# Output projection's weight sums: from accumulating DMAs to VectorE adds, two jobs behind their loads

## The chip, the cores and the metric

The kernel runs on one core of one Trainium2 chip. The metric is the device time of one execution in microseconds (us). Three runs of the kernel before gave a median of 634.77 us (634.74 to 635.29).

## The reference

One decoder block on 512 tokens of width 1024: RMSNorm, one input projection, an mLSTM branch (`ya`) and a sparse-attention branch (`yb`), each projected to width 1024, merged by sigmoid gates, then an output projection, a residual and a final RMSNorm. What matters here is the end:

```
merged = sigmoid(g_a) * (ya @ w_branch_a) + sigmoid(g_b) * (yb @ w_branch_b)
x = x + merged @ w_out
return rmsnorm(x, final_norm_g)
```

`w_branch_a` and `w_out` are 1024 x 1024, everything is float32, `merged` is 512 x 1024.

## The kernel before

**Products.** Each float32 operand is split into a high and a low part (`split`: ACT copies the high part to a rounded type, DVE subtracts it from the source), and a product is three matmuls: high by high, low by high, high by low.

**Branch A.** `branch(GA, j, ...)` computes the 128 columns of output block j for all 512 tokens: 8 x 3 = 24 matmuls into one PSUM bank of the ring `pp` (three banks). There are eight such jobs, in the order of blocks 0, 4, 1, 5, 2, 6, 3, 7; they are called jobs 1 to 8. A job's `load` asks SP for two things: the gate `s` (256 KB, ring of three buffers) and the weights `wr` (512 KB, ring of three), which are split at once into `wh` on ACT and `wl` on DVE (rings of four). The `Stream` loads two jobs ahead, so the load and the split of job k+2 are traced just before job k's matmuls. After the matmuls DVE does the *gating* of the job, `s = (s + 1) * bank`, and the *merge add*, `mB = s + mB`; the merge add frees the `s` buffer. `merge` then settles the block of the job before (`settle`: split into `meh` on ACT and `mel` on DVE), and after blocks 4, 5 and 6 forms sums of two blocks by four small DVE operations (`merged_sums`) and splits them into `mSh` and `mSl`.

**Output projection.** It is one level of Strassen-Winograd over quarters. The weights `w_out` fall into four quarters B11, B12, B21, B22 of 512 x 512, each in two tiles of 128 x 1024 numbers. Needed are also T3 = B12 + B22, T2 = T3 + B11, T4 = B21 + T2 and T1 = B11 + B12. Seven products follow in fixed order: M11 (with B11), M12 (B21), M22 (T4), MS2 (T2), MS3 (T3), MS1 (T1), MS4 (B22), 24 matmuls each. M11 reads blocks 0 to 3 of `merged` in turn, for tokens 0 to 127 and then 128 to 255; M12 blocks 4 to 7; M22 the other tokens.

**Weight sums before.** SP loads B12 straight into T3's tiles (`T`) and B22 into `R` tiles, and POOL issues two DMAs that accumulate B22 onto T3 (`added`). B11 is loaded, B12 a second time into `R` tiles, then B21. T2 is two DVE adds (`plus`), T1 two accumulating DMAs on POOL, T4 two DVE adds between M11 and M12 in the text. The calls `stream.run()`, which trace one job each, stand between these.

**What sets the order.** The text is traced once; the framework then places the instructions of each engine by its own estimate of when their operands are ready, earlier text first. Each engine and each DMA queue works its list strictly in order. `tc.keep_in_program_order(ins)` pins an instruction behind the one traced just before it on its engine. The set `ordered` names the engines on which all are pinned: it is emptied early in the kernel, and "pe" is added after the eight jobs, so in this stretch neither DVE nor ACT is pinned; SP and POOL never are.

Line 79 in the profile is the helper through which all PE, ACT and DVE instructions go, so tiles tell them apart. SP's loads are line 143 (weights), 1125 (`s`) and 1284 (`w_out`); POOL's accumulates are 1289 (weight sums) and 1330 (`aside`, output parts onto `xo`).

Of the kernel before, what the change touches and what calls it, by code (L numbers as in the profile page):

```python
# [15 lines left out]
OP = mybir.AluOpType  # L16
AX = mybir.AxisListType.X

T = 512
# [43 lines left out]
def build(  # L63
# [7 lines left out]
    class Engine:  # L71
# [3 lines left out]
        def __getattr__(self, op):  # L75
# [7 lines left out]

            return call

    pe, pool = Engine(nc.tensor, "pe"), nc.gpsimd
    act, dve = Engine(nc.scalar, "act"), Engine(nc.vector, "dve")
    A = act.activation
# [40 lines left out]
    def split(src, hi, lo, eng="a"):  # L129
        if eng == "a":  # L130
            A(hi, src, AF.Copy)
        elif eng == "p":
            pool.tensor_scalar(hi, src, 1.0, 1.0, OP.mult, OP.mult)
        else:
            dve.tensor_copy(hi, src)
        dve.tensor_tensor(lo, src, f(hi), OP.subtract)
# [3 lines left out]
    def weights(src, eng="a"):  # L140
        nk, n = src.shape[1], src.shape[2]
        raw = wp.tile([128, nk, n], F32, name="wr", tag="wr", bufs=3)
        nc.sync.dma_start(raw, src)
        hi = wp.tile([128, nk, n], F32R, name="wh", tag="wh", bufs=4)
        lo = wp.tile([128, nk, n], F32R, name="wl", tag="wl", bufs=4)
        split(raw, hi, lo, eng)
        return hi, lo
# [51 lines left out]
    def passes(ps, lh, ll, rh, rl, nk):  # L199
        for k in range(nk):  # L200
            a, b, c, d = lh(k), ll(k), rh(k), rl(k)
            pe.matmul(ps, a, c, start=k == 0, stop=False)
            yield
            pe.matmul(ps, a, d, start=False, stop=False)
            yield
            pe.matmul(ps, b, c, start=False, stop=k == nk - 1)
            if k < nk - 1:
                yield
# [17 lines left out]
    stream = Stream(2)  # L226
# [50 lines left out]
    def hilo(qs):  # L277
        out = []
        for q in qs:
            hi = wp.tile([128, 2, 512], F32R, name="wh", tag="wh", bufs=4)  # L280
            lo = wp.tile([128, 2, 512], F32R, name="wl", tag="wl", bufs=4)
            split(q, hi, lo)
            out.append((hi, lo))
        return out

    with tc.tile_pool(name="ph0", bufs=2, side="right") as p0, tc.tile_pool(
# [23 lines left out]
        for hf in range(2):  # L310
            ps = PS()
# [126 lines left out]
        split(b, *parts["S1"])  # L438
        split(d, *parts["S4"])

    def plus(dst, a, b):
        for d, x, y in zip(dst, a, b):
            dve.tensor_tensor(d, x, y, OP.add)
        return dst

    def product(banks, k, ws, start=True, tbs=(0, 1), cs=slice(0, 512)):
        ah, al = parts[k]
        for tb in tbs:
            ts = slice(tb * 128, tb * 128 + 128)
            for c in range(4):  # L450
                wh, wl = (w[:, c % 2, cs] for w in ws[c // 2])
                first, last = start and c == 0, c == 3
                m = lambda l, r, first=False, last=False: pe.matmul(
                    banks[tb][:, cs], l, r, start=first, stop=last, skip_group_check=True
                )
                m(ah[:, c, ts], wh, first)
                m(ah[:, c, ts], wl)
                m(al[:, c, ts], wh, False, last)
# [3 lines left out]
    def winograd(qs, target, sink, between=(), w1=None):  # L462
# [26 lines left out]
        Z = [PP() for _ in range(2)]  # L489
        w2 = hilo(b21)  # L490
        t3 = plus(WS(), b12, b22)
        do("t3")
        t2 = plus(WS(), t3, b11)
        do("t2")
        product(Z, "A12", w2)
# [7 lines left out]
        z = keep(X, "kz")  # L503
        w7 = hilo(t3)
        t4 = plus(t2, t2, b21)
        product(X, "S3", w7, False)
        do("P7")
# [130 lines left out]
    load = lambda: next(more)  # L638
# [467 lines left out]
    def branch(base, j, yh, yl, nk):  # L1106
        def gen(w):
            o = 0 if nk == ND else (j % 2) * 128
            ps = PP()
            yield from passes(  # L1110
                ps, lambda k: w[0][:, k, o : o + 128], lambda k: w[1][:, k, o : o + 128],
                lambda k: yh[:, k], lambda k: yl[:, k], nk,
            )
            s = halves.pop((base, j))
            if base == GB:
                if not merged:
                    merged.append(pers.tile([128, ND, T], F32, name="mB", tag="hTh"))
                dve.scalar_tensor_tensor(merged[0][:, j], s, 1.0, ps, OP.add, OP.mult)
            else:
                dve.scalar_tensor_tensor(s, s, 1.0, ps, OP.add, OP.mult)  # L1120
                merge(j, s)

        def load():
            halves[base, j] = sgp.tile([128, T], F32, name="s", tag="s")
            nc.sync.dma_start(halves[base, j], gD[base, j])
            if nk == ND:
                return weights(wav[:, :, j * 128 : j * 128 + 128])
            if j % 2 == 0:
                halves["w"] = weights(wbv[:, :, j * 128 : j * 128 + 256])
            return halves["w"]  # L1130

        stream.add(load, gen)
# [10 lines left out]
    for h in range(4):  # L1143
# [34 lines left out]
        for tb in range(NT):  # L1178
            po = PT()
            for sb in range(tb + 1):  # L1180
                a = KOFF[sb] + (tb - sb) * 128
# [49 lines left out]
    with tc.tile_pool(name="fin", bufs=1, reuse_waits="tile") as fp:  # L1231
# [10 lines left out]
        def merged_sums(i):  # L1242
            a, b = merged[0][:, i], merged[0][:, i + 4]
            a1, a2, b1, b2 = a[:, :256], a[:, 256:], b[:, :256], b[:, 256:]
            dve.tensor_tensor(b2, a2, b2, OP.subtract)
            dve.tensor_tensor(a2, a1, a2, OP.subtract)
            dve.tensor_tensor(a1, b2, a1, OP.subtract)
            dve.tensor_tensor(b1, a1, b1, OP.add)
            sums_split(i, a, 0)
# [9 lines left out]
        def settle():  # L1259
            j = waiting.popleft()  # L1260
            m = merged[0][:, j]
            split(m, meh[:, j], mel[:, j])
            return j

        def merge(j, s):
            m = merged[0][:, j]
            dve.tensor_tensor(m, s, m, OP.add)
            waiting.append(j)
            if len(waiting) > 1:
                k = settle()  # L1270
                if k in (4, 5, 6):
                    merged_sums(k - 4)
# [5 lines left out]
        def tiles(tag, bufs):  # L1278
            return [fp.tile([128, 2, 512], F32, name=tag, tag=tag, bufs=bufs) for _ in range(2)]

        def load(i, j, ts):
            for n, t in enumerate(ts):
                ks = slice(i * 4 + n * 2, i * 4 + n * 2 + 2)
                nc.sync.dma_start(t, wov[:, ks, j * 512 : j * 512 + 512])
            return ts

        def added(ts, more):
            for t, m in zip(ts, more):
                pool.dma_start(t, m, accum_op=OP.add)
            return ts  # L1290

        t3 = load(0, 1, tiles("T", 4))
        b22 = load(1, 1, tiles("R", 8))
        added(t3, b22)
        stream.run()
        b11 = load(0, 0, tiles("R", 8))
        stream.run()
        b12 = load(0, 1, tiles("R", 8))
        stream.run()
        b21 = load(1, 0, tiles("R", 8))  # L1300
        stream.run()
        t2 = plus(tiles("T", 4), t3, b11)
        stream.run(2)
        t1 = added(b12, b11)
        w1 = hilo(b11)
        stream.run()
        settle()
# [40 lines left out]
        L, R = slice(0, 512), slice(512, 1024)  # L1348
# [25 lines left out]
        aside(X, 0, 0, 0, 0.5)  # L1374
        Z = [PP() for _ in range(2)]
        t4 = plus(b21, b21, t2)
        w4 = hilo(t4)
        product(Z, "M12", w2)
        merged_sums(3)
# [65 lines left out]
```

## Time and profile before

| | |
|---|---|
| median of three runs | 634.77 us |
| profiled execution | 637.34 us, span of its instructions 635.3 us |
| mean granted TensorE clock | 0.992 |
| busy: PE, DVE, ACT, POOL | 96%, 78%, 54%, 9% |
| read from HBM | 62.35 MB |

One execution is recorded by the hardware profiler; times are from the span's start. A row of the timeline has start, length, engine, line, operation, output and inputs by tile names, the count, and in brackets how long the engine stood idle before it and what ended that. SPq and POOLq are the parts of those engines that issue DMAs. The "chain of waits" is followed back from the last instruction to what released each step.

### The profile page before, as it was taken

The page shows a single profiled execution, that of the slowest core. Times are in us where ns is not written, and L with a number is a line of the kernel's source. Part 1 is how long each engine was busy: PE and PEld are TensorE (multiplying, and loading weights), DVE is VectorE, ACT ScalarE, POOL GpSimd, SP SyncE. Part 2 cuts the span into 40 slices and gives each one's busy share as a digit, 9 for nine tenths or more (in the row PEclk, how much of TensorE's full clock was granted, in tenths as well). Part 3 has the DMA queues.
Part 4 walks back from the last instruction along what each step waited for, and adds up shares of the span by engine and source line. Part 5 has one row for each costly group of instructions (what it writes and reads, how often), then busy time and mean ns, then how long its engine had stood idle before and what let it go on. Part 6 is the DMA issues. An engine that isn't in the chain of part 4 may idle for free.

```text
span 635.3 us, 8633 instructions
## 1 busy us (share of the span) xinstructions
PE 608.0 (96%) x3014; PEld 502.5 (79%) x3014; DVE 494.0 (78%) x962; ACT 345.9 (54%) x650; POOL 59.1 (9%) x124
## 2 busy tenths in 40 slices
PE   5999999999999999999999999999999999987995
PEld 3988878888888877888888788887878788866784
DVE  4799979596685777876868676989898986459966
ACT  5645457554442456665665665666565643125564
POOL 4000000000000001221312130000000000100120
PEclk9999999999999999999999999999999999999898
DMA  7925644502067442131322213513232337993324
GB/s 240 336 92 165 214 134 122 173 5 83 18 176 197 107 127 83 51 84 50 84 57 77 84 39 97 146 36 99 67 100 67 100 116 200 297 249 105 111 50 150
DMA packets 83643, 76.02 MB, mean 120 GB/s; under 512 B 4960, under 2 KB 64516, under 8 KB 83600
## 3 DMA queue, kind: packets, MB, share of 16 engines
q1 hardware_dynamic: 82016, 71.53, 37.5%
q0 software_dynamic: 1440, 3.67, 3.3%
q8 instruction: 24, 0.39, 0.3%
q10 hardware_dynamic: 144, 0.26, 0.1%
q14 instruction: 19, 0.16, 0.1%
HBM read 62.35 MB, written 8.39 MB: 111 GB/s over the span
## 4 chain that ended last, share of the span: by engine, by line
PE 67%; DVE 16%; DMA 5%; ACT 5%; issue 4%; POOL 1%; SPq 1%; POOLq 0%; ACTq 0%; DVEq 0%
PE pp L79 38%; PE ps L79 16%; PE pt L79 10%; PE po L79 3%; DVE u L79 3%; DVE wl L79 2%; ACT wh L79 2%; DMA T<-R 1%; DMA R<-w_out 1%; DVE mB L79 1%; DMA wr<-w_branch_a 1%; DVE Dm L79 1%; DMA xt<-x 1%; DVE Sl L79 1%; DVE Th L79 1%
## 5 line engine op out<-in xcount | busy, mean ns | idle before, releaser
L79 PE MATMUL pp<-hTh,wh 128*128 128x512 f32 (+1 forms) x360 | 142.6, 396 | 0.0
L79 PE MATMUL pp<-hTl,wh 128*128 128x512 f32 (+1 forms) x360 | 140.0, 389 | 0.0
L79 PE MATMUL pp<-hTh,wl 128*128 128x512 f32 (+1 forms) x360 | 139.8, 388 | 0.0
L79 ACT ACTIVATE wh<-wr 128x1024 fp32r<-128x1024 f32 x56 | 59.0, 1058 | 59.2 <-PE pp L79 43.9
L79 DVE TENSOR_TENSOR wl<-wr,wh 128x1024 fp32r<-128x1024 f32 x56 | 68.2, 1219 | 17.0 <-ACT wh L79 16.9
L79 PEld LDWEIGHTS pp<-hTh,wl 128*128 128x128 f32 x360 | 67.7, 188 | 13.1
L79 PEld LDWEIGHTS pp<-hTh,wh 128*128 128x128 f32 x360 | 67.8, 188 | 10.6
L79 PEld LDWEIGHTS pp<-hTl,wh 128*128 128x128 f32 x360 | 67.9, 189 | 9.9
L959 POOL TENSOR_SCALAR P<-P,st 128x128 f32<-128x128 f32 (+1 forms) x64 | 34.6, 560 | 160.9 <-DVE st L79 69.0
L79 DVE TENSOR_TENSOR wl<-R,wh 128x1024 fp32r<-128x1024 f32 x28 | 33.9, 1221 | 12.8 <-ACT wh L79 12.7
L79 DVE TENSOR_TENSOR wl<-T,wh 128x1024 fp32r<-128x1024 f32 x28 | 33.8, 1222 | 10.4 <-ACT wh L79 10.4
L79 ACT ACTIVATE P<-P,st 128x128 f32<-128x128 f32 (+3 forms) x64 | 35.5, 555 | 11.2 <-DVE st L79 10.7
L79 ACT ACTIVATE pth<-pt 128x512 fp32r<-128x512 f32 (+1 forms) x64 | 26.9, 434 | 25.9 <-PE pt L79 14.6
L79 DVE TENSOR_TENSOR ptl<-pt,pth 128x512 fp32r<-128x512 f32 (+1 forms) x64 | 29.9, 485 | 14.2 <-ACT pth L79 13.7
L79 DVE CUSTOM_DVE_ANT_0 P<-ps,cst 128x128 f32<-128x128 f32 (+3 forms) x64 | 30.5, 487 | 12.7 <-PE ps L79 12.5
L79 ACT ACTIVATE wh<-R 128x1024 fp32r<-128x1024 f32 x28 | 29.1, 1054 | 16.3 <-PE pt L79 7.1
L79 DVE SCALAR_TENSOR_TENSOR u<-pp,prm,u 128x511 f32<-128x511 f32 (+2 forms) x48 | 35.7, 744 | 0.2
L79 ACT ACTIVATE wh<-T 128x1024 fp32r<-128x1024 f32 x28 | 29.1, 1055 | 12.1 <-PE ps L79 5.6
L79 PE MATMUL ps<-k,Th 128*128 128x256 f32 (+2 forms) x112 | 29.1, 341 | 1.4 <-PE pp L79 0.8
L79 PE MATMUL pt<-cst,P 128*128 128x128 f32 x160 | 28.4, 277 | 0.9 <-DVE ptl L79 0.8
L79 PEld LDWEIGHTS pt<-cst,P 128*128 128x128 f32 x160 | 19.7, 140 | 10.9 <-DVE ptl L79 5.8
L79 PE MATMUL pp<-yah,wh 128*128 128x512 f32 x64 | 25.0, 391 | 2.1 <-ACT wh L79 2.1
(350 smaller groups left out, 1392.6 us busy)
## 6 DMA issues: line engine op xcount, KB each, us to landing
wr<-w_in SPq DMA_DIRECT2D x44, 512.0 KB, 4.0
R<-w_in SPq DMA_DIRECT2D x24, 512.0 KB, 4.6
gD<-sg SPq DMA_DIRECT2D x16, 256.0 KB, 2.0
s<-gD SPq DMA_DIRECT2D x16, 256.0 KB, 5.8
wr<-w_branch_a SPq DMA_DIRECT2D x8, 512.0 KB, 4.1
R<-w_out SPq DMA_DIRECT2D x8, 512.0 KB, 9.5
vD<-cq SPq DMA_DIRECT2D x8, 256.0 KB, 3.7
wr<-vD SPq DMA_DIRECT2D x4, 512.0 KB, 4.1
```

The source lines that it names most:

```text
L79: ins = fn(*args, **kw)
L959: pool.tensor_scalar(pj, pj, st[:, 2, j : j + 1], 1.0, OP.mult, OP.mult)
```

## The change

T3 is now computed by DVE from B12 and B22, which are each loaded once into `R` tiles. The loads stand one job apart (B12 before job 1, B22 after it, B11 after job 2, B21 after job 4); T3's adds are traced after job 3, T2's after job 5, and both pairs are pinned. T1 is still accumulated by POOL's DMAs, but traced after T4's adds. The gating and the merge add of the branch-A jobs are pinned too, so each gating stands behind the DVE instruction traced just before it.

```
+    keep = tc.keep_in_program_order
...
-    def plus(dst, a, b):
+    def plus(dst, a, b, held=lambda ins: ins):
         for d, x, y in zip(dst, a, b):
-            dve.tensor_tensor(d, x, y, OP.add)
+            held(dve.tensor_tensor(d, x, y, OP.add))
         return dst
...
-                dve.scalar_tensor_tensor(s, s, 1.0, ps, OP.add, OP.mult)
+                keep(dve.scalar_tensor_tensor(s, s, 1.0, ps, OP.add, OP.mult))
                 merge(j, s)
...
-            dve.tensor_tensor(m, s, m, OP.add)
+            keep(dve.tensor_tensor(m, s, m, OP.add))
...
-        t3 = load(0, 1, tiles("T", 4))
+        b12 = load(0, 1, tiles("R", 8))
+        stream.run()
         b22 = load(1, 1, tiles("R", 8))
-        added(t3, b22)
         stream.run()
         b11 = load(0, 0, tiles("R", 8))
         stream.run()
-        b12 = load(0, 1, tiles("R", 8))
+        t3 = plus(tiles("T", 4), b12, b22, keep)
         stream.run()
         b21 = load(1, 0, tiles("R", 8))
         stream.run()
-        t2 = plus(tiles("T", 4), t3, b11)
-        stream.run(2)
-        t1 = added(b12, b11)
+        t2 = plus(tiles("T", 4), t3, b11, keep)
+        stream.run()
         w1 = hilo(b11)
         stream.run()
         settle()
...
         t4 = plus(b21, b21, t2)
+        t1 = added(b12, b11)
         w4 = hilo(t4)
```

## The prediction

> **What bounds the kernel now.** I read the busy table and the chain of waits first, then the PE rows from 568 us on, then the DVE and SP rows just ahead of each PE stall, and last tables by stage. Jobs are numbered by order: branch-A job 1 is output block 0, then blocks 4, 1, 5, 2, 6, 3, 7 are jobs 2 to 8.
>
> ```profile
> span 635.3 us, 8633 instructions
> PE 608.0 (96%) x3014; PEld 502.5 (79%) x3014; DVE 494.0 (78%) x962; ACT 345.9 (54%) x650; POOL 59.1 (9%) x124
> ...
> PE 67%; DVE 16%; DMA 5%; ACT 5%; issue 4%; POOL 1%; SPq 1%; POOLq 0%; ACTq 0%; DVEq 0%
> ```
>
> TensorE is the bound over the whole span; a change to the weight sums can only win where PE stands still. The timeline of PE shows that place (start, length, idle before it and its releaser):
>
> ```profile
> 567.96 0.39 PE L79 MATMUL pp<-yah,wl 128*128 128x512 f32 x1
> 570.41 0.50 PE L79 MATMUL pp<-yah,wh 128*128 128x512 f32 x1 [2.07 <-ACT wh L79]
> 571.67 0.50 PE L79 MATMUL pp<-yah,wl 128*128 128x512 f32 x1 [0.53 <-DVE wl L79]
> ...
> 584.04 0.39 PE L79 MATMUL ps<-wh,mel 128*128 128x512 f32 x1
> 587.61 0.80 PE L79 MATMUL ps<-wh,meh 128*128 128x512 f32 x1 [3.18 <-ACT meh L79]
> ...
> 594.22 0.40 PE L79 MATMUL pp<-wh,meh 128*128 128x512 f32 x1
> ...
> 599.70 0.39 PE L79 MATMUL pt<-wh,meh 128*128 128x512 f32 x1
> ...
> 605.14 0.39 PE L79 MATMUL ps<-wh,mSh 128*128 128x512 f32 x1
> ```
>
> From 599.70 to 605.14 PE runs the 24 matmuls of M22 without a stop: 5.44 us, 0.227 each. Job 6's last matmul starts at 567.96, so job 7 was due at 568.19. Between 568.19 and 599.70 stand 96 matmuls (jobs 7 and 8, M11, M12), 21.76 us of work in 31.51 us. **PE loses 9.75 us here**: 2.07 and 0.53 because job 7's weights are late, 3.18 because block 3 of the merged activations is late, and then a slow clock: from 587.61 to 594.22 the 15 remaining matmuls of M11 take 6.61 us instead of 3.40, so 3.21 more. The other 0.76 is pipeline restart around the three gaps.
>
> Why are the weights and block 3 late? The DVE timeline:
>
> ```profile
> 541.18 0.69 DVE L79 SCALAR_TENSOR_TENSOR s<-s,pp 128x512 f32<-128x512 f32 x1 [3.35 <-PE pp L79]
> ...
> 552.57 1.23 DVE L79 TENSOR_TENSOR T<-T,R 128x1024 f32<-128x1024 f32 x1 [8.23 <-DMA T<-R]
> 553.71 0.68 DVE L79 SCALAR_TENSOR_TENSOR s<-s,pp 128x512 f32<-128x512 f32 x1
> ...
> 555.44 0.68 DVE L79 TENSOR_TENSOR mB<-s,mB 128x512 f32<-128x512 f32 x1
> ...
> 570.39 1.23 DVE L79 TENSOR_TENSOR wl<-wr,wh 128x1024 fp32r<-128x1024 f32 x1 [6.61 <-ACT wh L79]
> ...
> 574.70 0.68 DVE L79 SCALAR_TENSOR_TENSOR s<-s,pp 128x512 f32<-128x512 f32 x1
> ...
> 585.01 0.68 DVE L79 SCALAR_TENSOR_TENSOR s<-s,pp 128x512 f32<-128x512 f32 x1
> ```
>
> The gatings (`s<-s,pp`) are those of jobs 1, 2, 5 and 7. At 24 matmuls a job, PE finished job 2 at about 546.4, job 5 at 562.7. Gating 2 starts 7 us late: ahead of it in DVE's queue stood the first add of T2 = T3 + B11, which waited 8.23 us for the DMA that accumulates B22 onto T3. Its releaser, in the chain of waits:
>
> ```profile
> 534.65 8.60 DMA R<-w_out
> ...
> 543.88 8.66 DMA T<-R
> ```
>
> A load of 8.60 us, then an accumulate of 8.66. The late gating then goes round through SP (and ACT, last row):
>
> ```profile
> 533.69 0.91 SPq L1284 DMA_DIRECT2D T<-w_out  x2
> ...
> 536.46 1.08 SPq L1125 DMA_DIRECT2D s<-gD  x1
> ...
> 543.01 0.98 SPq L1284 DMA_DIRECT2D R<-w_out  x2
> 556.15 0.34 SPq L1125 DMA_DIRECT2D s<-gD  x1
> 556.53 1.85 SPq L1284 DMA_DIRECT2D R<-w_out  x2
> 558.49 0.53 SPq L143 DMA_DIRECT2D wr<-w_branch_a  x1
> 560.34 3.59 SPq L1125 DMA_DIRECT2D s<-gD  x1
> 564.03 0.39 SPq L143 DMA_DIRECT2D wr<-w_branch_a  x1
> ...
> 569.30 1.06 ACT L79 ACTIVATE wh<-wr 128x1024 fp32r<-128x1024 f32 x1 [7.80 <-DMA wr<-w_branch_a]
> ```
>
> The `s` ring has three buffers; job 5's sits in SP's queue until job 2's merge (555.44 + 0.68) frees one at 556.12. Quarter B21 and job 7's weights stand behind it. Those weights are asked for at 558.49 and split at 569.30, 10.8 us later, on a crowded DMA. DVE's second stall (6.61) is this same load, with gating 5 queued behind it 12 us after its matmuls. From there DVE has a backlog that puts gating 7 at 585.01, 8.6 us after PE finished job 7, and M11 stops on block 3. One cause, all 9.75 us.
>
> **The change part by part.** DMA first: the queues in a window, then two stages (us, PE, PEld, DVE, ACT, POOL busy, clock, DMA share).
>
> ```profile
> DMA packets 5926, 9.62 MB, mean 278 GB/s; under 512 B 331, under 2 KB 2225, under 8 KB 5924
> q1 hardware_dynamic: 5348, 7.50, 64.3%
> q0 software_dynamic: 576, 2.10, 34.0%
> ...
> 533.60:568.20 34.60, 34.60 (x154) 28.41 (x152) 16.90 (x24) 7.57 (x10) 3.70 (x4) 1.00 0.99 278
> 568.20:599.70 31.50, 25.73 (x97) 19.88 (x97) 28.57 (x43) 16.59 (x23) 1.74 (x2) 0.89 0.45 133
> ```
>
> The DMA engines are full (0.99) from 533.6 to 568.2. Plain transfers took 64.3% of 34.6 us, 22.2 us for 7.50 MB: 3.0 us per MB. POOL's four accumulates (T3's two, T1's two) took 34.0%, 11.8 us for 2.10 MB: 5.6 us per MB.
>
> *Removed.* The second load of B12 (two SP issues, 1.05 MB): 3.1 us of DMA time. T3's accumulate (two POOL issues, 1.05 MB): 5.9 us. So 9.0 of 34.6 us of DMA work go, and the full stretch should end near 559 instead of 568. The 8.23 us DVE wait goes with them. What is late next: the plain loads of B12 and B22.
>
> *Added.* T3 = B12 + B22 on DVE: two adds of 1.23, so 2.45 us. They are pinned behind the last DVE instruction traced before them, the merged-sum split of jobs 1 and 2, which can't precede merge 2, about 547.9. Loads asked for from 533.7 to 538 and landing in 8.60 are there by 547. I take no wait.
>
> *Moved: T2's adds*, same two, now behind the split that follows job 4 (PE end 557.3). B11 is then asked for behind job 4's `s`, about 543, and is there by 552. *B22, B11 and B21* go one job later in program order, so in SP's queue each may stand one `s` further back: B22 behind 536.5, B11 behind 542.6, B21 behind merge 2 or 3 (547.9 or 553.4). Even the last leaves B21 twenty us before its split.
>
> *Weights.* With merge 2 at 547.9 instead of 556.1, job 7's weights are asked for between 550 and 556. Charged with the worst landing above, 10.8, they come at 561 to 567; with 7.54, the chain's price for job 8's, at 558 to 564. PE needs them split (1.06 + 1.23) at 568.2, so landed by 565.9. I take 562, the 7.54 from the middle of that window, since the DMA is less full than when 10.8 was paid: both first gaps go.
>
> *Pinned gating.* Each gating now can't pass the instruction traced just before it, which is the weight split of the job two later (or a quarter's split); the merge add is pinned behind the gating. That wait is new by name; the 570.39 row shows that the order was already so there. Queued behind it are merge, `s` load and weights. With weights at 562, gating 5 (PE end 562.7) waits at most about 2 us, and the PSUM bank it holds is wanted by job 8 only at 573.6: hidden. Uncovered, it costs what the 570.39 row costs.
>
> *T1's accumulate* is traced after T4's adds, on POOL, which has nothing else from 547 to 592; it may float up as soon as T3 has read B12, or stand beside the first output accumulates. It is wanted by the split at 609.47, 9.75 earlier in new time, 599.7. Bounds: 0 to 0.87 (one POOL issue ahead of the output accumulates, their row below), or a gain of its 5.9 us of DMA time off the full stretch. I take 0.
>
> ```profile
> 609.47 1.06 ACT L79 ACTIVATE wh<-R 128x1024 fp32r<-128x1024 f32 x1 [0.81 <-PE ps L79]
> ...
> 592.54 0.87 POOL L1330 DMA_DIRECT2D xo<-late  x1 [34.89 <-ACT late L79]
> ```
>
> *Is DVE able to carry it?* Its busy time from job 1's gating until T4's splits are done:
>
> ```profile
> 541.10:568.20 27.10, 14.23 (x21) 1.00 1.00 279
> 568.20:597.90 29.70, 26.84 (x40) 0.89 0.47 139
> ```
>
> 41.07 us, with T3 43.5. New time allows 541.1 to 588.15, 47.05 us. It fits with 3.5 us to spare, so DVE is 92% loaded and its order matters. I give back one wait of the smallest size seen, 0.53.
>
> **Sum.** 9.75 - 0.53 = 9.2 us. Against the profiled execution, 637.34 us (span 635.3): 628.1. That execution stands 2.57 above the median 634.77; nothing in its rows says the 9.75 would differ, so on the median: **625.5 us**.
>
> A page on the clock: the Trainium skill, TensorE: Matmul & The Clock Gate, section What's actually happening, puts the drop to half clock after at least one idle window of about 3.4 us. Here 2.07 us of idle left the clock alone and 3.18 cost it. By that rule 3.18 is a borderline case, and an execution that escaped it would have 3.2 less to win, 628.7. The three runs lie within 0.6 us of each other, so I go by the row. It also says that a leftover wait near 2 us should stay cheap.
>
> **The rivals.** *A, partial:* the weights are on time, but DVE's 92% is met in a bad order and M11 still stops for block 3. For it: the 3.5 us of slack, and gating 7 standing behind both splits of B11. Against: block 3 is not wanted until 9 matmuls into M11, 581.1, 7.5 us after job 7's end. If all of 3.18 + 3.21 and its restart stay, only some 3.0 of the 9.75 is won, 631.8; if under 2 us, about 627.
>
> *B, no change:* DVE waits for a plain w_out load where it waited for the accumulate. The load alone took 8.60. For it to hold gating 2 back as before, B22 would have to land near 552, so be asked for at 543 or later, and T3 would have to stand before gating 2, which its pin forbids. 634.8.
>
> *C, slower:* the pin ties gating to weights and the three `s` buffers tie weights to gating. If SP keeps job 7's weights behind job 7's `s`, they wait for merge 4 (558.8): landing with 10.8 at 570, gating 5 after their split, 572.3; merge 5 at 573.6 frees job 8's `s` and weights, landing with 7.54 at 581.5, split 583.8. Job 7 runs from 572.3 (4.1 us idle, half clock, 3.2 more), job 8 from 583.8 to 589.3, M11 and M12 to 600.2, and T2's 2.45 now lies inside the jam: 602.6 against 599.70, so about 637.7. It decides when job 7's weights land after about 569. Against: before, they were asked for ahead of the `s` of two jobs, and the DMA has 9.0 us less to do.
>
> **How the numbers follow.** Full recovery 0.53 (its own range 623.8 to 627.0); A 0.23 (627 to 633.4); B 0.09; C 0.15. 0.2% of 634.8 is 1.3 us, about what measurement tells from no change: faster 0.76, same 0.09, slower 0.15. Below, at most one more wait could go with fewer transfers, DVE's for an output accumulate:
>
> ```profile
> 622.14 0.42 DVE L79 SCALAR_TENSOR_TENSOR xo<-pp,xo 128x256 f32<-128x256 f32 x1 [1.67 <-DMA xo<-late]
> ```
>
> 625.5 less 1.67 is 623.8. Above, the range takes in A and the better half of B: 634.9.
>
> **What would show it.** Right: no `T<-R` on POOL; two `T<-R,R` adds after 548 with little idle; gating 2 near 547; job 7's weights asked for before 557; no PE idle over 1 us from 568 to 600; M22 starting near 590 and no 0.43 us spacing in M11. Wrong: DVE idle of several us before a weight split or a T add, with a gating right behind it; SP holding weights behind an `s` load past 558; an `meh` wait still in M11; or T1's accumulate among the output accumulates with DVE waiting on `xo<-late`.

## The result and the profile after

| | before | after |
|---|---|---|
| median, us | 634.75 (633.47 to 635.29, 4 runs) | 626.14 (625.76 to 626.62, 4 runs) |
| ratio | | 0.9868, 95% interval 0.985 to 0.9885 |
| profiled execution; span, us | 637.34; 635.3 | 626.62; 624.8 |
| mean granted clock | 0.992 | 0.997 |
| read from HBM | 62.35 MB | 61.30 MB |

The forecast was 625.5 us; the measurement stands 0.6 us above it. From the page of the changed kernel, the busy table and the chain's shares by engine:

```profile
span 624.8 us, 8626 instructions
PE 604.0 (97%) x3014; PEld 501.3 (80%) x3014; DVE 496.2 (79%) x964; ACT 345.5 (55%) x650; POOL 57.5 (9%) x122
...
PE 75%; DVE 13%; ACT 5%; issue 3%; DMA 1%; POOL 1%; SPq 0%; POOLq 0%; ACTq 0%; DVEq 0%
```

DMA's share of the chain falls from 5% to 1%, PE's rises from 67% to 75%. The chain of waits (start, length, engine or transfer) now runs through the whole branch A on PE:

```profile
532.63 46.28 PE pp L79 x204
578.91 5.44 PE ps L79 x24
584.35 5.44 PE pp L79 x24
```

M11 (`ps`) and M12 (`pp`) take 5.44 us each, which is 24 matmuls at 0.227, and M22 (`pt`) follows. From job 1's gating to the first matmul of M22 before needed 599.70 - 541.18 = 58.52 us. The timeline of the changed kernel shows 589.63 - 540.87 = 48.76 us, 9.76 less:

```profile
540.87 0.69 DVE L79 SCALAR_TENSOR_TENSOR s<-s,pp 128x512 f32<-128x512 f32 x1 [3.35 <-PE pp L79]
...
546.31 0.69 DVE L79 SCALAR_TENSOR_TENSOR s<-s,pp 128x512 f32<-128x512 f32 x1 [2.29 <-PE pp L79]
...
548.66 1.04 SPq L144 DMA_DIRECT2D wr<-w_branch_a  x2
...
552.75 1.22 DVE L79 TENSOR_TENSOR T<-R 128x1024 f32<-128x1024 f32 x1
...
554.56 1.08 POOL L1290 DMA_DIRECT2D R<-R  x1 [27.69 <-DVE mB L79]
554.59 12.23 SPq L1126 DMA_DIRECT2D s<-gD  x3
...
555.86 1.06 ACT L79 ACTIVATE wh<-wr 128x1024 fp32r<-128x1024 f32 x1 [3.83 <-DMA wr<-w_branch_a]
...
561.02 1.21 DVE L79 TENSOR_TENSOR wl<-wr,wh 128x1024 fp32r<-128x1024 f32 x1
...
564.59 0.68 DVE L79 SCALAR_TENSOR_TENSOR s<-s,pp 128x512 f32<-128x512 f32 x1
...
566.39 2.35 DVE L79 TENSOR_TENSOR T<-T,R 128x1024 f32<-128x1024 f32 x2
...
578.78 0.68 DVE L79 TENSOR_TENSOR mel<-mB,meh 128x512 fp32r<-128x512 f32 x1
...
581.24 0.39 PE L79 MATMUL ps<-wh,mel 128*128 128x512 f32 x1
...
589.63 0.39 PE L79 MATMUL pt<-wh,meh 128*128 128x512 f32 x1
```

Gating 2 starts at 546.31 with PE's matmul as its releaser, not the accumulate (553.71 before). T3's adds (`T<-R`) wait for nothing. The weights of jobs 7 and 8 are asked for together at 548.66 (before: 558.49 and 564.03), those of job 7 are split at 555.86 (before 569.30). Job 8's now also stand ahead of job 6's `s` in SP's list (554.59); before, they stood behind it. Job 8's split starts on DVE at 561.02, and gating 5 behind it at 564.59 (before 572.77 and 574.70). Block 3's low part is done at 578.78 + 0.68 = 579.46, 1.78 us ahead of the matmul that reads it, 581.24. T1's two accumulates stand on POOL at 554.56, and nobody waits for them. The windows (us, PE, PEld, DVE, ACT, POOL busy, clock, DMA share, GB/s):

```profile
533.60:560.00 26.40, 26.40 (x118) 21.84 (x117) 17.07 (x24) 9.31 (x11) 1.95 (x2) 1.00 0.95 287
560.00:568.20 8.20, 8.20 (x38) 6.80 (x37) 8.06 (x13) 3.68 (x6) 0.00 (x0) 1.00 0.42 96
568.20:590.00 21.80, 21.80 (x98) 18.07 (x97) 21.35 (x31) 10.88 (x15) 1.74 (x2) 1.00 0.45 149
```

PE is busy without a stop. In windows of 1 us the DMA is full until 561 (1.09 from 560 to 561, then 0.72); before, it was full until 570 (1.19 from 569 to 570, then 0.55). DVE has 0.45 us left in the last window.

### The profile page after: what moved, and what is told of

Same layout as the page of the kernel before. It is cut to its first block, busy times and chain, and to the rows that moved or that the text cites. A ratio compares the mean times of both kernels' runs of the same rounds, so it can differ in the third digit from the quotient of the medians.

```text
span 624.8 us, 8626 instructions
## 1 busy us (share of the span) xinstructions
PE 604.0 (97%) x3014; PEld 501.3 (80%) x3014; DVE 496.2 (79%) x964; ACT 345.5 (55%) x650; POOL 57.5 (9%) x122
## 3 DMA queue, kind: packets, MB, share of 16 engines
HBM read 61.30 MB, written 8.39 MB: 112 GB/s over the span
## 4 chain that ended last, share of the span: by engine, by line
PE 75%; DVE 13%; ACT 5%; issue 3%; DMA 1%; POOL 1%; SPq 0%; POOLq 0%; ACTq 0%; DVEq 0%
PE pp L79 45%; PE ps L79 17%; PE pt L79 10%; PE po L79 3%; DVE u L79 3%; DVE wl L79 2%; ACT wh L79 1%; DVE Dm L79 1%; DMA xt<-x 1%; DVE Sl L79 1%; DVE Th L79 1%; DVE xo L79 1%; DVE qkl L79 1%; DVE P L79 1%; DVE num L79 1%
## 5 line engine op out<-in xcount | busy, mean ns | idle before, releaser
L79 DVE TENSOR_TENSOR wl<-wr,wh 128x1024 fp32r<-128x1024 f32 x56 | 68.1, 1217 | 10.5 <-ACT wh L79 10.5
L79 DVE TENSOR_TENSOR wl<-R,wh 128x1024 fp32r<-128x1024 f32 x28 | 33.9, 1219 | 10.5 <-ACT wh L79 10.4
L79 DVE TENSOR_TENSOR wl<-T,wh 128x1024 fp32r<-128x1024 f32 x28 | 33.8, 1221 | 10.4 <-ACT wh L79 10.3
L79 PEld LDWEIGHTS pt<-cst,P 128*128 128x128 f32 x160 | 19.7, 140 | 10.8 <-DVE ptl L79 5.8
L79 PE MATMUL pp<-yal,wh 128*128 128x512 f32 x64 | 24.9, 389 | 0.0
```

What stands on the lines that cost most here:

```text
L79: ins = fn(*args, **kw)
```

## The experiments

Each kernel was measured against the kernel before on the same chip. Three groups shared such runs; the kernel before had medians of 635.51, 635.57 and 635.54 us in them. The theory at the start was the prediction's chain: T2's add waits for the accumulate, that holds gating 2, that holds the `s` buffer, that holds the weights. The main rival was that the weights are late because of the transfers in front of them, wherever the adds stand. In the table the times from the profiled execution are: start of job 8's `wl` split on DVE, of gating 5, of block 3's `mel`, and the stretch from job 1's gating to M22. In all kernels job 7's split stands ahead of job 8's on DVE, and gating 5 behind both.

| kernel | median us | ratio (95%) | job 8 `wl` | gating 5 | block 3 | stretch |
|---|---|---|---|---|---|---|
| before | 634.75 | 1 | 572.77 | 574.70 | 587.95 | 58.52 |
| after | 626.14 | 0.9868 (0.985 to 0.9885) | 561.02 | 564.59 | 578.78 | 48.76 |
| before, T2's adds later | 634.05 | 0.998 (0.9965 to 0.9996) | 569.90 | 571.84 | 586.36 | 57.27 |
| before, `s` loads on POOL | 633.84 | 0.9952 (0.9922 to 0.9983) | 570.38 | 573.50 | 586.74 | 56.53 |
| before, weights asked first | 626.84 | 0.9865 (0.985 to 0.988) | 558.51 | 563.02 | 576.55 | 48.76 |
| after, idle load and accumulate | 634.73 | 0.9989 (0.9979 to 0.9998) | 569.92 | 571.86 | 586.39 | 56.54 |
| after, idle load | 632.48 | 0.9934 (0.9913 to 0.9955) | 567.46 | 569.40 | 583.92 | 55.04 |
| after, idle accumulate | 635.73 | 1.0004 (0.9984 to 1.0025) | 566.98 | 570.56 | 584.75 | 55.90 |
| after, adds at the loads | 627.01 | 0.9868 (0.9854 to 0.9883) | 563.14 | 567.65 | 579.96 | 48.76 |
| after, T2 added three times | 627.3 | 0.9865 (0.985 to 0.988) | 560.67 | 564.24 | 580.54 | 49.16 |
| after, T2 added five times | 633.52 | 0.9973 (0.9959 to 0.9987) | 560.23 | 563.80 | 584.63 | 53.21 |

**The kernel before, measured once more.**

> The kernel before once more, for a second profile of it. Theory (one chain: accumulate, T2's add, gating 2, s buffer, job 7's weights, gating 5, block 3): the same three PE gaps of about 2.1, 0.5 and 3.2 us and about 3.2 us of half clock in M11, 634.8 us. Rival: the profiled execution of before, 637.3, was an odd one, and the half clock or one of the gaps is smaller here; then the span is about 633 instead of 635.3.

Median 635.45, ratio 1.0004 (0.9992 to 1.0016). The same picture in another execution, span 633.5: gaps of 1.87 and 0.52 before job 7, then

```profile
585.93 0.80 PE L79 MATMUL ps<-wh,meh 128*128 128x512 f32 x1 [3.19 <-ACT meh L79]
```

and half clock behind it (matmuls 0.43 apart). The loss is no accident of one execution.

**The pins.** The gating and the merge add are no longer pinned.

> The changed kernel without the pins on gating and merge add. Listed engine by engine, its instructions stand in the same order as with the pins. Theory: the pins do nothing here, 626.1 us within 0.5. Rival: the pins carry part of the gain, above 627.5.

```
-                keep(dve.scalar_tensor_tensor(s, s, 1.0, ps, OP.add, OP.mult))
+                dve.scalar_tensor_tensor(s, s, 1.0, ps, OP.add, OP.mult)
...
-            keep(dve.tensor_tensor(m, s, m, OP.add))
+            dve.tensor_tensor(m, s, m, OP.add)
```

Median 626.09, ratio 0.9855 (0.984 to 0.987), and every engine has the same list of instructions. The pins fix an order that the framework chooses anyway.

**T2's adds alone moved.** The kernel before, with T2's adds pinned behind job 5; both accumulates and the second B12 load stay.

> The kernel before with one thing moved: T2's two adds are traced and pinned after job 5; T3 is still accumulated by POOL's DMAs and B12 loaded twice. Theory that the place of T2's adds in DVE's queue is the cause: gating 2 near 547, job 7's weights asked for near 550 and landed by 562, no PE gap over 1 us before M22, 626 to 627.5 us. Rival that the 9 us of DMA work are the cause: job 7's weights still land near 568 on a full DMA, DVE waits for them, 630 to 635.

```
-        t2 = plus(tiles("T", 4), t3, b11)
-        stream.run(2)
+        stream.run()
+        t2 = plus(tiles("T", 4), t3, b11, keep)
+        stream.run()
```

634.05 us: the prediction's first link is taken away and almost nothing is won. Its timeline:

```profile
546.37 0.69 DVE L79 SCALAR_TENSOR_TENSOR s<-s,pp 128x512 f32<-128x512 f32 x1 [2.29 <-PE pp L79]
...
549.30 0.46 SPq L144 DMA_DIRECT2D wr<-w_branch_a  x1
...
566.49 1.06 ACT L79 ACTIVATE wh<-wr 128x1024 fp32r<-128x1024 f32 x1 [11.72 <-DMA wr<-w_branch_a]
...
585.42 0.50 PE L79 MATMUL ps<-wh,meh 128*128 128x512 f32 x1 [3.79 <-ACT meh L79]
```

Gating 2 is prompt and job 7's weights are asked for at 549.30, 9.2 us earlier than before, but they are split at 566.49, only 2.8 us earlier. They took 17.2 us. The DMA was full either way, and asking earlier bought little.

**The `s` loads on another queue.** Those of jobs 5 to 8 are issued by POOL, so SP's weights no longer stand behind them.

> The kernel before, sums and accumulates untouched; only the s loads of branch-A jobs 5 to 8 are issued by POOL instead of SP, so B21 and job 7's and 8's weights no longer stand behind them in SP's list. T2's first add still waits for T3's accumulate, with gating 2 behind it. Theory now held (a full DMA serves weights in the order they were asked for; PE loses time when job 7's weights land after 566): weights asked for near 544, ahead of T1's accumulates, landed by 560; DVE's wait for T3 stays at 8 us but PE has no gap over 1 us; 626 to 628 us. Rival (T2's wait itself costs the 9 us): 633 to 636.

```
-            nc.sync.dma_start(halves[base, j], gD[base, j])
+            queue = nc.gpsimd if base == GA and j in (2, 6, 3, 7) else nc.sync
+            queue.dma_start(halves[base, j], gD[base, j])
```

```profile
545.89 10.25 SPq L143 DMA_DIRECT2D wr<-w_branch_a  x2
...
570.38 1.23 DVE L79 TENSOR_TENSOR wl<-wr,wh 128x1024 fp32r<-128x1024 f32 x1 [5.54 <-ACT wh L79]
...
586.40 0.80 PE L79 MATMUL ps<-wh,meh 128*128 128x512 f32 x1 [4.31 <-ACT meh L79]
```

A miss: median 633.84, inside the range that the expectation gave to its rival. The two weight issues alone kept SP for 10.25 us, and job 8's weights, which landed 21.9 us after they were asked for, still held DVE until 570.38. T2's wait is there too (8.28 us), so this run does not decide between the two; the run above and the one with the removed DMA work put back, below, do. Its ten executions run from 626.6 to 635.4, and why they differ so much is not known. The Trainium skill, DMA: Bandwidth & Descriptors, section Issuing engines are not separate DMA queues, says that loads started by different engines end on the same 16 DMA engines, and that another queue saves only issue time. The run agrees: the DMA share is 1.02 from 533.6 to 560 and 1.03 to 568.2.

**Place of the adds.** The changed kernel with the loads in the old order, T3's adds straight behind B22's load and T2's behind B11's.

> The changed kernel with T3's and T2's adds traced right behind their loads (loads in the old order) instead of two jobs later. In the listed order T2's first add again stands ahead of gating 2, now behind plain loads. Theory (the accumulate made the wait long, and PE stops only once job 7's weights land after 566): DVE waits some 3 to 5 us for B22 and B11, gating 2 at 549 to 552, weights still in time, 626 to 627.5 us. Rival B of the prediction: the wait moves to the loads and costs the same, 633 to 635.

```
         b12 = load(0, 1, tiles("R", 8))
-        stream.run()
         b22 = load(1, 1, tiles("R", 8))
+        t3 = plus(tiles("T", 4), b12, b22, keep)
         stream.run()
         b11 = load(0, 0, tiles("R", 8))
...
+        t2 = plus(tiles("T", 4), t3, b11, keep)
+        stream.run(2)
         b21 = load(1, 0, tiles("R", 8))
```

627.01 us and no gap on PE. "Two jobs behind" is not needed; the weights come in time here too (job 8's split at 563.14). DVE waited only 0.40 us for a load, and gating 2 stands at 548.57.

**T1 by VectorE too.**

> The changed kernel with T1 also added by DVE, pinned behind T4's adds: no accumulate is left among the weight sums, DVE does 2.4 us more just ahead of T4's splits. Theory (DVE's order has a little to spare there: T4's second split is wanted 1.4 us into M22): no PE gap over 0.5 us, 625.6 to 626.8 us. Rival (DVE is the bound by now): M22 waits some 2 us, 627.5 to 628.5.

```
-        t1 = added(b12, b11)
+        t1 = plus(b12, b12, b11, keep)
```

626.63 us, ratio 0.985 (0.9833 to 0.9866). T1's accumulate costs the changed kernel nothing that can be measured.

**The removed DMA work put back, read by nobody.** The changed kernel, plus a second load of B12 into spare `T` tiles and B22 accumulated on them.

> The changed kernel with its old DMA work put back as an idle copy: B12 is loaded a second time into T tiles and B22 accumulated onto it, and nobody reads the result. Theory of the DMA backlog: job 7's weights, asked for near 549, land near 565 instead of 556, DVE stalls before their split, M11 stops again: 632 to 636 us. Rival (T2's wait for the accumulate is the cause): gating 2 stays near 547 and nothing is lost, 626 to 627.

```
+        added(load(0, 1, tiles("T", 4)), b22)
```

```profile
550.06 0.95 SPq L144 DMA_DIRECT2D wr<-w_branch_a  x1
...
566.14 1.06 ACT L79 ACTIVATE wh<-wr 128x1024 fp32r<-128x1024 f32 x1 [11.14 <-DMA wr<-w_branch_a]
567.24 1.23 DVE L79 TENSOR_TENSOR wl<-wr,wh 128x1024 fp32r<-128x1024 f32 x1 [8.86 <-ACT wh L79]
...
585.45 0.79 PE L79 MATMUL ps<-wh,meh 128*128 128x512 f32 x1 [4.17 <-ACT meh L79]
```

634.73 us: all of the gain is gone, although no sum waits for these transfers and gating 2 is prompt (546.09). Job 7's weights, asked for only 1.4 us later than in the changed kernel, are split 10.3 us later. Job 8's stand behind job 6's `s` again and are asked for at 555.40, but they are split behind job 7's in any case. What the change bought it bought in the landing of these weights, not in T2's wait.

**The same DMA work, in another order.** The kernel before with T2's adds moved as above, and B21 and the second B12 asked for only behind all weights of branch A.

> All the DMA work of the kernel before stays (second load of B12, both accumulates); T2's adds stand behind job 5 on VectorE as in the run with T2 later, and the loads of B21 and the second B12 are asked for only behind the weights of jobs 7 and 8. Theory (a weight load lands when what was asked ahead of it on the full DMA has drained): the weights of job 7 land by about 557 us instead of 566, gating 5 is no longer held, block 3 is in time, no PE gap over 0.5 us before 600, 626 to 627.5 us. Rival (the amount of DMA work in the stretch sets the time, whatever its order): the sums come late instead, 632 to 635 us.

```
         b11 = load(0, 0, tiles("R", 8))
-        stream.run()
-        b12 = load(0, 1, tiles("R", 8))
-        stream.run()
-        b21 = load(1, 0, tiles("R", 8))
-        stream.run()
-        stream.run()
+        stream.run(4)
         t2 = plus(tiles("T", 4), t3, b11, keep)
         stream.run()
+        b21 = load(1, 0, tiles("R", 8))
+        b12 = load(0, 1, tiles("R", 8))
```

Its timeline and its windows:

```profile
542.47 0.39 SPq L144 DMA_DIRECT2D wr<-w_branch_a  x1
...
554.35 1.06 ACT L79 ACTIVATE wh<-wr 128x1024 fp32r<-128x1024 f32 x1 [2.60 <-DMA wr<-w_branch_a]
...
556.82 1.06 ACT L79 ACTIVATE wh<-wr 128x1024 fp32r<-128x1024 f32 x1 [0.89 <-DMA wr<-w_branch_a]
```

```profile
533.60:560.00 26.40, 26.40 (x118) 21.89 (x117) 17.13 (x25) 9.67 (x12) 1.95 (x2) 1.00 1.03 321
560.00:568.20 8.20, 8.20 (x38) 6.80 (x37) 7.82 (x12) 3.32 (x5) 1.74 (x2) 1.00 0.97 221
```

626.84 us, as good as the change, with the second load and both accumulates still there. The DMA is full to 568 (1.03, 0.97), as before, but PE does not stop: the weights are split at 554.35 and 556.82. T1's accumulates, too, come later here (POOL issues them at 560.99 and 563.32, behind the late B12). So the amount of DMA work is not the harm, and neither is an accumulate as such: T3's still runs beside job 7's weights, which took 11.9 us but were asked for at 542.47. The harm is in how late the weights are asked for and how much stands ahead of them then.

**Half of the DMA work put back.** First the load alone, then one accumulate alone, onto spare tiles that POOL sets to zero.

> The changed kernel with B12 loaded a second time and read by nobody: 1.05 MB, about 3.1 us more DMA work ahead of the weights of job 7, no accumulate. Theory: the weights land at about 559 to 560 us instead of 556, still ahead of the 566 from which gating 5 is late: no PE gap, 626 to 627.5 us. Rival (any added DMA work moves the end in proportion, a third of the 8 us between the kernels): 628.5 to 630 us.

```
+        load(0, 1, tiles("T", 4))
```

> The changed kernel with one accumulating transfer of 1.05 MB into spare tiles that nothing reads, about 5.9 us of DMA work, no second load. Theory: the weights of job 7 land at about 561 to 562 us, VectorE stands still for 4 to 5 us at their split, which its spare time still takes up: 626 to 628.5 us. Rival (an accumulate is the whole harm by itself, since it slows every other transfer while it runs): weights after 565, 632 us or more.

```
+        spare = tiles("T", 4)
+        for t in spare:
+            pool.memset(t, 0.0)
+        added(spare, b22)
```

Both were misses: 632.48 and 635.73 us. The load alone:

```profile
549.14 0.41 SPq L144 DMA_DIRECT2D wr<-w_branch_a  x1
554.56 0.34 SPq L1126 DMA_DIRECT2D s<-gD  x1
554.99 0.39 SPq L144 DMA_DIRECT2D wr<-w_branch_a  x1
...
566.37 1.06 ACT L79 ACTIVATE wh<-wr 128x1024 fp32r<-128x1024 f32 x1 [7.13 <-DMA wr<-w_branch_a]
567.46 1.23 DVE L79 TENSOR_TENSOR wl<-wr,wh 128x1024 fp32r<-128x1024 f32 x1 [6.70 <-ACT wh L79]
...
584.66 0.80 PE L79 MATMUL ps<-wh,mel 128*128 128x512 f32 x1 [0.94 <-DVE mel L79]
```

The load did more than fill the DMA for some 3 us: it also moved SP's list on by a place, so that job 8's weights now stand behind job 6's `s`, which waits for a buffer until 554.56. They are asked for 5.8 us later than in the changed kernel and land after 11.3 us, while job 7's are split at 556.39, only 0.5 us later than there. This is also the order of the kernel before (its SP rows at 558.49, 560.34 and 564.03). So part of what the change won probably came from this list: with one load fewer, job 8's weights moved ahead of job 6's `s`. How much the place alone is worth, without the added 1.05 MB, was not tried. The accumulate alone left SP's list as it was:

```profile
547.55 5.73 SPq L144 DMA_DIRECT2D wr<-w_branch_a  x2
553.29 0.87 POOL L1290 DMA_DIRECT2D R<-R  x1 [8.82 <-DVE T L79]
...
558.45 1.06 ACT L79 ACTIVATE wh<-wr 128x1024 fp32r<-128x1024 f32 x1 [7.63 <-DMA wr<-w_branch_a]
...
565.88 1.06 ACT L79 ACTIVATE wh<-wr 128x1024 fp32r<-128x1024 f32 x1 [5.85 <-DMA wr<-w_branch_a]
...
583.81 0.79 PE L79 MATMUL ps<-wh,meh 128*128 128x512 f32 x1 [4.07 <-ACT meh L79]
```

I had looked at job 7's weights, and these came at 558.45, earlier than expected. Job 8's came at 565.88. After DVE's waits of 5.56 and 3.29 us ahead of the two splits, gating 5 is at 570.56, 6 us late in an execution that started 1.2 us earlier. The delay of job 8's weights, some 8 us, is more than the 5.9 us that the accumulate itself takes. In the same stretch T1's accumulates (553.29) run beside those weights, while in the changed kernel they start as the weights land. That they are the rest of the delay is argued from these rows, not tried. The expectation's rival, that an accumulate slows every other transfer while it runs, named such a time (632 us or more); the run with the weights first speaks against it as the whole harm, but whether an accumulate slows its neighbours more than a load does stays open. Nor is it explained why the ten executions reach from 632.9 to 638.2, with the recorded one the fastest.

**How much room DVE has.** T2's adds repeated: four more (4.9 us), then eight more (9.8 us).

> The changed kernel with T2's two adds done three times over (four extra adds of 1.22, 4.9 us more on DVE at about 568). Prediction's budget: 3.5 us to spare, so PE should wait 1 to 2 us in M11 for block 3, 627 to 628.5 us; if that wait exceeded 3 us, half clock would add 3 more, 632. Rival (DVE has far more room than the budget says): 626.

> The changed kernel with eight more adds of T2's kind on VectorE (9.8 us), the result unchanged in place but not in value (B12 is added five times). Theory: VectorE has about 5 us to spare, so block 3's gated tile comes about 5 us late, PE stands for about 5 us ahead of M11 and then runs some 6 us at half clock (3.2 us lost): 633 to 636 us. Rival (late only by what is over the spare time, no loss of clock): 631 to 632 us. A third: other waits take it up, under 629 us.

```
+        for _ in range(2):      # range(4) in the second kernel
+            plus(t2, t3, b11, keep)
```

Each repeat forms the same sum again, so the remark on its value in the second expectation is mistaken. Measured: 627.3 and 633.52 us. In the first, block 3's low part moved only from 578.78 to 580.54, since the framework set other DVE work behind it; the stretch grew by 0.4 us, in pieces too small for the timeline to flag. In the second (timeline):

```profile
565.61 11.44 DVE L79 TENSOR_TENSOR T<-T,R 128x1024 f32<-128x1024 f32 x10
...
580.04 0.50 PE L79 MATMUL ps<-wl,meh 128*128 128x512 f32 x1 [1.07 <-DVE wl L79]
...
583.63 0.50 PE L79 MATMUL ps<-wh,meh 128*128 128x512 f32 x1 [1.49 <-ACT meh L79]
...
585.38 0.50 PE L79 MATMUL ps<-wh,mel 128*128 128x512 f32 x1 [1.01 <-DVE mel L79]
```

block 3 is 5.9 us late and PE stands in three places, 3.57 us together, at full clock (the next matmul follows after 0.34 us and the rest 0.23 apart; the window from 580 to 588 has a clock of 1.00). The time fell into the range named for the theory, but not by its working: in this execution (632.76 us) no half clock followed.

**The room at block 3.** In the changed kernel block 3's low part is ready 1.78 us before PE wants it. Take how much later than 578.78 it comes, corrected for the start of job 1's gating, less 1.78: for the idle accumulate 5.97 + 1.21 - 1.78 = 5.4 us, for the idle load 5.14 + 0.04 - 1.78 = 3.4, for T2 three times 1.76 + 0.22 - 1.78 = 0.2. The matmul that reads it (581.24 in the changed kernel) started at 585.49, 584.66 and 581.27, which with the same correction is 5.5, 3.5 and 0.3 us late. So in these runs M11 is late by what block 3 is late beyond this room.

## Why the prediction was right, and where its working was not

**The 9.75 us of loss on PE, all to be won: right.** The stretch shrank by 9.76 us. No gap from job 7 to M22 is left, and the clock stays at 1.00.

**The 0.53 given back for a DVE wait: not seen.** That the sum came within 0.6 us of the median is in part luck. The profiled execution of before, 637.34 us, lay above all four timed runs (633.47 to 635.29); the one recorded again took 635.44, with a span of 633.5. From one profiled execution to the other the span fell by 10.5 us, the medians by 8.6. The prediction carried the 9.2 of one execution over to the median; the 0.53 made that error smaller.

**9.0 us of DMA work removed, full stretch to end 9 us earlier: right,** and it was the term that mattered. The stretch ended 9 us earlier, though at 561 instead of 570, both 2 us later than forecast. DMA share from 560 to 568.2 fell to 0.42.

**"One cause", the late gating 2: the step that failed.** The prediction let the accumulate act through DVE's list and the `s` buffers: gating 2 late, so weights asked for late. With gating 2 prompt but the DMA work kept, the weights were asked for 9.2 us earlier and the kernel won 0.2% (0.04 to 0.35). With T3 and T2 formed on DVE and the DMA work put back, it won 0.1%. With the DMA work kept and the weights asked for ahead of it, everything was won. The accumulate and the extra load did their harm on the DMA, ahead of the weights of jobs 7 and 8, and the extra load, as the idle-load run suggests, also by its place in SP's list. The change takes away the late gating and the DMA work together, so the forecast of the time could come out although its cause was wrong; that is luck. No run has gating 2 late by 7 us with the DMA work gone, so whether the late gating alone would have cost anything stays open.

**The weights' landing: right in effect, wrongly bounded.** The forecast took 562 and called 10.8 us the worst landing; job 7's came by 555.86. In the runs with the DMA work ahead of them the same load took 17.2 us, so 10.8 bounded nothing. The forecast also gave 565.9 as the latest landing, from PE's need of job 7's weights, and did not follow job 8's. The tighter limit is job 8's split, which stands ahead of gating 5: at 563.14 or earlier on DVE the time was 626 to 627.3 us (unless DVE itself was loaded), at 566.98 or later 632.5 or more. This is a comparison of the rows of the table, not a run of its own.

**Rival A (partial, by DVE's order)** did not come true, but the room was smaller than said: not 3.5 us of budget, but 1.78 us at block 3 for a wait that the framework does not foresee. **Rival B (DVE waits for plain loads)** did not occur: even with the adds straight behind the loads the wait was 0.40 us. **Rival C (SP keeps the weights behind `s`)** did not occur in the changed kernel, but it names a real danger: in the run with the idle load job 8's weights slipped behind one `s`, and with that, and the added load, the kernel lost 4 us of its 8.6 by the ratios of the table, 6 by the medians.

**The pins, T3's adds, T1's accumulate at nothing: right,** each seen by itself in a run or a row above.

## What to carry to other kernels

When a load lands late, look at what was asked for ahead of it on the full DMA before blaming the instruction that waited. Moving the request earlier past a wait won 0.2% here; moving it ahead of two other loads (2.1 MB, and T1's accumulates came later with them), or taking 9 us of transfers away, won 1.3%. Find the last landing whose consumer stands in front of the critical work in an in-order list (here job 8's weights in front of gating 5) and keep its slack in view, for the load of a tight engine tells only an average. One load more or less can also shift a queue's list by a place, in an experiment as in the change itself, so compare the lists before reading a transfer as time alone.

## What the runs showed of the hardware

An issue can hold the issuing engine: two weight issues kept SP for 10.25 us in the run with the `s` loads on POOL, 1.04 in the changed kernel. The DMA was busy in both (share 1.06 and 0.98 from 545.9 to 556), so that alone does not do it; how much must be queued before an issue holds its engine, no run here shows. And the landing time of one and the same load, job 8's 512 KB of weights, went from 8.2 us (changed kernel) to 17.5 us (idle accumulate) and 21.9 us (`s` loads on POOL). In that order, from the views of the two jobs' weights and from the chain of waits:

```profile
DMA to landing us min/median/max: 7.1/7.7/8.2
...
DMA to landing us min/median/max: 10.8/14.2/17.5
...
547.25 21.93 DMA wr<-w_branch_a
```

On the clock: an idle time of 3.01 us flagged in two pieces (2.07 and 0.94, ending 1.7 us apart) was followed by half clock (granted clock 0.50 from 584.6 to 590.3), as this timeline of the idle-load run shows; matmuls are 0.43 apart:

```profile
585.25 0.63 PE L79 MATMUL ps<-wh,meh 128*128 128x512 f32 x1
585.68 0.63 PE L79 MATMUL ps<-wl,meh 128*128 128x512 f32 x1
```

Before job 7 in the kernel before, 2.07 and 0.53 were not, nor were 1.07, 1.49 and 1.01 over 6.4 us in the run with T2 added five times. That last kernel's ten executions differ: three at 632.6 to 632.8 us had mean clocks of 0.995 to 0.997, the other seven took 633.3 to 636.0 at 0.988 to 0.995. The Trainium skill, TensorE: Matmul & The Clock Gate, section What's actually happening, names a window of about 3.4 us that runs free of the kernel, so that one kernel can meet it differently from run to run. The spread agrees with that; that the window is its cause is not shown. The drop after 3.01 us in two pieces, with two matmuls between them, does not look like one wholly idle window of 3.4 us. The drop after 3.18 us in one piece (before) is short of it too, but the ends of matmuls in a trace are modelled, so it says less.
